# The last low part of the fetched weights written behind the copies of the turned exponentials, in five steps of the attention over the neighbourhoods

## The chip, the core and the metric

The kernel runs on one core of a Trainium2 chip. The metric is the device time of one execution in microseconds (us). Names of engines: PE is TensorE's matmul side and PEld its weight loads, DVE is VectorE, ACT is ScalarE, POOL is GpSimd, SP is SyncE, which issues the weight transfers.

## The reference

Two layers of a transformer over 256 latent tokens and 256 context tokens of width 1024: the first mixes with a retention, the second with attention over neighbourhoods, and each is followed by a squared-ReLU MLP. The change lies in the second layer's attention: 32 heads of 32, the latent tokens on a grid of 4 rows by 64 columns, each query with 8 x 16 neighbours at most (here all 4 rows) and all 256 context tokens. Cut to what matters:

```python
q = p[..., :d].reshape(b, rows, GRID_W, nh, hd) * scale
s_loc = jnp.einsum('bqhd,bikhd->bhqik', q_r, k_band).astype(jnp.float32) + bias
s_ctx = jnp.einsum('bqhd,blhd->bhql', q_r, k_c).astype(jnp.float32)
s = jnp.concatenate([s_loc.reshape(b, nh, GRID_W, band), s_ctx], axis=-1)
prob = jax.nn.softmax(s, axis=-1).astype(v.dtype)
o = (jnp.einsum('bhqik,bikhd->bqhd', p_loc, v_band)
     + jnp.einsum('bhql,blhd->bqhd', prob[..., band:], v_c))
y_lat = o.reshape(b, n, d) @ w_o
```

## The kernel before

**Split operands.** Matmul operands of 32-bit floats are held as two parts: a high part that ScalarE casts (`hi`) and a low part that VectorE makes as the difference (`lo = raw - hi`). A product is then three matmuls: high by high, high by low, low by high (`mm3`).

**Weights.** They come in units of 512 KB in a fixed order. `fetch(n)` (line 255) issues the transfers of the next n units on SP into one of four `raw` buffers and writes the ScalarE casts of their high parts at once; the VectorE subtractions are put on a list, `pending`. `lows(n)` (line 277) writes the first n of that list. `take(n)` (line 282) hands units to a product. A `raw` buffer comes free when its subtraction has run, and SP's queue, which runs in order, waits for that before a later transfer. There are five buffers each for high and low parts.

**Banks.** PSUM has eight banks, handed out by `bank()` (line 156). One is held for the attention's sums (`pav`); the other seven serve in turn the scores (`pqk`, four a step), the projections (`pn`, `pnv`, `pnw`) and the transposes (`ppt`, four a step). A matmul into a bank waits until the evacuation of its former contents has run.

**The order.** PE, ACT and DVE run in the order in which the code is written (`ORDER`, line 1396); SP too. The attention goes over sixteen pairs n of a head group and a half of the queries; the loop at line 1825 has thirteen steps, and step n works on three pairs at once:

- `gather(n + 1)` on POOL: small copies of exponentials, and the transfers of bias rows; `turned(n)`: an ACT copy of the inverted sums.
- `scores(n + 2)` on PE: twelve score matmuls into four banks.
- `soften(n + 2)`: on DVE, four times, the bias added and the extreme found (`s`, `mn`), then on ACT four exponentials with their sums.
- `fetch(late)` and `lows(late)`: up to two units of weights.
- `run(before)`: a projection: K gives `kT` (ACT casts its high part, DVE subtracts for the low one), Q gives `qT` the same way in two pieces, V is copied by ACT, W is the output projection (`pnw`).
- `flip(n + 1)`: thirteen transposes of the exponentials on PE into four banks, which ACT (first and third) and DVE (second and fourth) copy to `pt`, 384 or 512 columns each.
- `invert(n + 2)` on DVE: reciprocal of the sums and its spread (`rr`).
- `fetch(last)`, then `attend(n)`: PE multiplies `pt` with V into `pav`, DVE scales it (`rt`), ACT casts the high part `oTh`, DVE subtracts for `oTl`. At the end of a step what is left on the list is written.

The table `STEPS` (line 1805) gives each step its numbers early, late and last and its projections: steps 1, 2 and 4 have late = 2 with K(3), K(4) and Q(2), step 3 has late = 1 with K(5), and step 9 has late = 2 with Q(3) and K(6). Step 5 has late = 1 with V(0).

Of the kernel before, what the change touches and what calls it, by code (L numbers as in the profile page):

```python
# [104 lines left out]
def kernel(  # L105
# [46 lines left out]
    def nm(s):  # L152
        uid[0] += 1
        return f"{s}_{uid[0]}"

    def bank(s="ps"):
        return psp.tile([P, 512], F32, tag="ps", name=nm(s))
# [8 lines left out]
    def tsl(t):  # L166
        return slice(t * P, (t + 1) * P)
# [87 lines left out]
    def fetch(n, in_scratch=False, at=None):  # L255

        for src, k, ncol in specs[len(units) : len(units) + max(n, 0)]:
            raw = rawp.tile([P, k, ncol], F32, tag="raw", name=nm("raw"))
            sp.dma_start(out=raw[:], in_=src.rearrange("(k p) n -> p k n", p=P))
            if in_scratch or len(units) in scratch_units:  # L260
                hi, lo = Rows([scr("hi", F32R) for _ in range(k)]), Rows([scr("lo", F32R) for _ in range(k)])
                for i in range(k):
                    act.copy(out=hi[:, i, :], in_=raw[:, i, :])
                    pending.append((lo[:, i, :], raw[:, i, :], hi[:, i, :]))
                units.append((hi, lo))
                continue
            if at is None:
                hi = hip.tile([P, k, ncol], F32R, tag="hi", name=nm("hi"))
                lo = lop.tile([P, k, ncol], F32R, tag="lo", name=nm("lo"))
            else:  # L270
                both = slot(at, [P, 2, k, ncol], F32R, "hilo")
                hi, lo = both[:, 0], both[:, 1]
            act.copy(out=hi[:], in_=raw[:])
            pending.append((lo[:], raw[:], hi[:]))
            units.append((hi, lo))

    def lows(n=100, eng=None):
        for lo, raw, hi in pending[:n]:
            (eng or dve).tensor_sub(out=lo, in0=raw, in1=hi.bitcast(F32))
        del pending[:n]  # L280

    def take(n, ahead=WB, open_=0):
        first = taken[0]
        while len(units) < min(first + max(n, ahead), len(specs)):
            fetch(1)
            lows()
        taken[0] = first + n
        assert len(units) - len(pending) >= first + n - open_
        return units[first : first + n]
# [987 lines left out]
    for hf in range(2):  # L1277
# [65 lines left out]
        for half in range(2):  # L1343
# [24 lines left out]
            held = take(4)  # L1368
# [174 lines left out]
    def scores(n):  # L1543

        g, qt = n // 2, n % 2
        pss[n] = [bank("pqk") for _ in range(4)]
        q, k = q_of(g), kTs[g // 2][:, g % 2]
        for i, (a, b) in enumerate(((0, 0), (0, 1), (1, 0))):
            for j in range(4):
                js = slice(32 * j, 32 * j + 32)  # L1550
                pe.matmul(
                    pss[n][j][:], lhsT=q[js, a, tsl(qt)], rhs=k[js, b, :], start=(i == 0), stop=(i == 2),
                    tile_position=(32 * j, 0),
                )

    def soften(n):

        mn = smp.tile([P, 4], F32, tag="mn", name=nm("mn"), bufs=3)
        sm = sums[n] = smp.tile([P, 4], F32, tag="sums", name=nm("sums"), bufs=3)
        for j in range(4):  # L1560
            s = Es[n, j] = scr("s")
            dve.tensor_tensor_reduce(
                out=s[:].rearrange("p (a t) -> p a t", a=2),
                in0=pss[n][j][:].rearrange("p (a t) -> p a t", a=2),
                in1=bias_ap(n, j),
                scale=1.0,
                scalar=3.0e38,
                op0=ALU.add,
                op1=ALU.min,
                accum_out=mn[:, j : j + 1],  # L1570
            )
            act.activation(
                out=s[:], in_=s[:], func=AF.Exp, scale=-1.0, bias=mn[:, j : j + 1], accum_out=sm[:, j : j + 1]
            )
# [7 lines left out]
    def invert(n):  # L1582

        rr = rrs[n] = smp.tile([P, 4, HD], F32, tag="rr", name=nm("rr"), bufs=1)
        dve.reciprocal(out=sums[n][:], in_=sums[n][:])
        dve.tensor_copy(out=rr[:], in_=sums[n][:].unsqueeze(2).broadcast_to([P, 4, HD]))
# [6 lines left out]
    def pt_at(n, i):  # L1593
        return turns[n % 2][:, tsl(i)]

    def gather(n):

        o = 0 if n % 2 else P
        c0 = 24 if n % 2 else 0
        for j in range(4):  # L1600
            pool.tensor_copy(
                out=pt_at(n, RAW)[:, 32 * j : 32 * j + 32].rearrange("p (r c) -> p r c", r=4),
                in_=Es[n, j][:, o : o + P].rearrange("p (r c) -> p r c", r=4)[:, :, c0 : c0 + 8],
            )
        if n + 2 < NS:
            load_bias(n + 2)

    def flip(n, sums_too=True):
        for j in range(4):
            pp = bank("ppt")  # L1610
            for i, kc in enumerate((n % 2, 2, 3)):
                pe.transpose(pp[:, tsl(i)], Es[n, j][:, tsl(kc)], ident)
            w = 3 * P
            if j == 3:
                pe.transpose(pp[:, tsl(3)], pt_at(n, RAW), ident)
                w = 4 * P
            (dve.tensor_copy if j % 2 else act.copy)(
                out=turns[n % 2][:, 3 * j * P : 3 * j * P + w], in_=pp[:, :w]
            )
        if sums_too:  # L1620
            flip_sums(n)

    def flip_sums(n):
        pe.transpose(av_half(n)[:, P:], rrs[n][:].rearrange("p h d -> p (h d)"), ident)
# [4 lines left out]
    def turned(n):  # L1629

        rts[n] = smp.tile([P, P], F32, tag="rt", name=nm("rt"), bufs=2)
        act.copy(out=rts[n][:], in_=av_half(n)[:, P:])

    def attend(n):

        g, qt = n // 2, n % 2
        oTh, oTl = oTs[0]
        po, rt = av_half(n), rts[n]
        pe.matmul(po[:, :P], lhsT=rest_values(n), rhs=pt_at(n, NEAR), start=True, stop=False)
        for i, kc in enumerate((qt, 2, 3)):  # L1640
            for j in range(4):
                pe.matmul(
                    po[32 * j : 32 * j + 32, :P],
                    lhsT=vtile(kc, g // 4)[:, (4 * (g % 4) + j) * HD : (4 * (g % 4) + j + 1) * HD],
                    rhs=pt_at(n, 3 * j + i),
                    start=False,
                    stop=(i == 2),
                    tile_position=(0, 32 * j),
                )
        dve.tensor_mul(out=rt[:], in0=po[:, :P], in1=rt[:])  # L1650
        hi, lo = (
            o[:, g].rearrange("p (r b c) -> p r b c", r=4, b=2)[:, :, qt] for o in (oTh, oTl)
        )
        split(rt[:].rearrange("p (r c) -> p r c", r=4), hi, lo)
# [166 lines left out]
    def run(fs):  # L1821
        for f in fs:
            f()

    for n, (early, late, last, before, after) in enumerate(STEPS):
        gather(n + 1)
        turned(n)
        fetch(early)
        lows(early)
        scores(n + 2)  # L1830
        soften(n + 2)
        fetch(late)
        lows(late)
        run(before)
        flip(n + 1)
        invert(n + 2)
        fetch(last)
        attend(n)
        run(after)

        lows(100 if n < len(STEPS) - 2 else len(STEPS) - 1 - n)


    n = NS - 1
# [263 lines left out]
    held = {}  # L2108
# [105 lines left out]
```

## Time and profile before

| | us |
|---|---|
| three runs | 1179.67, 1178.79, 1179.38; median 1179.38 |
| the profiled execution | 1179.48 |
| its span, first to last instruction | 1177.4 |
| mean granted TensorE clock, share of full speed | 0.998 |
| step 2, from flip to flip (859.33 to 868.44) | 9.11 |
| step 3 (868.44 to 877.72) | 9.28 |
| step 4, with the two pieces of Q (877.72 to 887.74) | 10.02 |
| step 5 (887.74 to 897.36) | 9.62 |
| step 6 (897.36 to 906.50) | 9.14 |

Times in the profile count from the start of the span. The span is that of one execution; about 2.1 us lie around it. In a timeline a row has the start, the length of the row, the engine, the operation, what it writes and reads (out<-in) and how many instructions follow each other (x), and in brackets the idle time of the engine before it with what ended that. A row of several instructions is as long as all of them. Reads of an accumulator are left out of what is shown. A stage above starts with the transposes of one flip and ends with those of the next, so it holds the scores and the projection of the step that gives it its name.

### The profile page before, as it was taken

The numbers are of one execution on the slowest core, as the hardware profiler recorded it, in microseconds if no ns is written. First come the engines' busy times: TensorE is split into PE (matmuls) and PEld (weight loads), VectorE is DVE, ScalarE is ACT, GpSimd is POOL, SyncE is SP. The second block draws the span as 40 slices with busy tenths as digits, with TensorE's granted clock in tenths as the row PEclk, the third lists the DMA queues.
The fourth block names the chain that finished last, engine by engine and source line by source line (L and its number), as shares of the span: only waits on it lengthen the run. The fifth ranks groups of instructions, "written<-read, shape, count | busy, mean of one in ns | idle before, by whom it ended". The sixth has DMA issues, their size and how long they took to land.

```text
span 1177.4 us, 17745 instructions
## 1 busy us (share of the span) xinstructions
PE 1167.3 (99%) x6821; PEld 985.6 (84%) x6821; DVE 844.6 (72%) x1349; ACT 480.6 (41%) x819; POOL 212.5 (18%) x364
## 2 busy tenths in 40 slices
PE   9999999999999999999999999999999999999997
PEld 7788888888888889888888888889888878999886
DVE  3786678787888787757767675678577589877446
ACT  3643332222323246442212333137466666665341
POOL 0103001000200241780203000223343430000001
PEclk9999999999999999999999999999999999999999
DMA  9943544544355416757566665646344334766660
GB/s 276 276 130 104 161 143 140 152 147 152 118 169 175 141 60 214 189 112 217 171 190 197 212 199 190 201 141 204 83 135 139 111 115 155 222 209 197 233 212 36
DMA packets 140115, 195.10 MB, mean 166 GB/s; under 512 B 9936, under 2 KB 81136, under 8 KB 140032
## 3 DMA queue, kind: packets, MB, share of 16 engines
q1 hardware_dynamic: 131904, 182.03, 49.4%
q0 software_dynamic: 6976, 9.39, 3.9%
q10 hardware_dynamic: 1152, 2.56, 0.7%
q8 instruction: 53, 0.87, 0.3%
q14 instruction: 30, 0.25, 0.1%
HBM read 189.12 MB, written 5.75 MB: 166 GB/s over the span
## 4 chain that ended last, share of the span: by engine, by line
PE 94%; DMA 2%; SPq 1%; ACT 1%; DVE 1%; issue 0%; POOL 0%; ACTq 0%; DVEq 0%
PE p L84 44%; PE pw L84 7%; PE pg L84 7%; PE pq L84 7%; PE pv L84 7%; PE pn L84 5%; PE pnv L84 4%; PE po L84 3%; PE ppt L84 2%; PE pnw L84 1%; PE pS L84 1%; PE pav L84 1%; PE pqk L84 1%; SPq L84 1%; PE pt L84 1%; PE p1t L84 1%
## 5 line engine op out<-in xcount | busy, mean ns | idle before, releaser
L84 ACT CAST hi<-raw 128x1024 fp32r<-128x1024 f32 (+2 forms) x228 | 231.7, 1032 | 308.9 <-PE p L84 113.4
L84 DVE TENSOR_TENSOR lo<-raw,hi 128x1024 fp32r<-128x1024 f32 (+2 forms) x228 | 273.4, 1213 | 105.5 <-ACT hi L84 105.4
L84 PE MATMUL p<-hi,hid 128*128 128x512 f32 (+1 forms) x832 | 241.8, 373 | 0.0
L84 PEld LDWEIGHTS p<-hi,hid 128*128 128x128 f32 x832 | 152.1, 188 | 27.6
L84 PE MATMUL p<-hTh,lo 128*128 128x256 f32 (+1 forms) x512 | 165.8, 326 | 0.0
L84 PE MATMUL p<-hTl,hi 128*128 128x256 f32 (+1 forms) x512 | 165.8, 326 | 0.0
L84 PE MATMUL p<-hTh,hi 128*128 128x256 f32 (+1 forms) x512 | 162.9, 328 | 0.0
L84 PE MATMUL p<-lo,hid 128*128 128x512 f32 (+1 forms) x416 | 155.2, 373 | 0.0
L84 DVE SCALAR_TENSOR_TENSOR acc<-rawa,scol,acc 128x1024 f32<-128x1024 f32 x56 | 74.5, 1342 | 66.0 <-DMA rawa<-in_ada_w_dram 66.0
L84 PEld LDWEIGHTS p<-hTh,lo 128*128 128x128 f32 x512 | 96.4, 188 | 8.8
L84 PEld LDWEIGHTS p<-hTl,hi 128*128 128x128 f32 x512 | 96.4, 188 | 8.7
L84 PEld LDWEIGHTS p<-hTh,hi 128*128 128x128 f32 x512 | 94.2, 188 | 8.7
L84 PEld LDWEIGHTS p<-lo,hid 128*128 128x128 f32 x416 | 78.4, 188 | 13.7
L84 DVE SCALAR_TENSOR_TENSOR strips<-rawa,scol,strips 128x512 f32<-128x512 f32 x112 | 78.6, 762 | 0.0
L84 ACT CAST hid<-r 128x256 fp32r<-128x256 f32 (+1 forms) x64 | 31.9, 500 | 111.2 <-DVE r L84 111.2
L84 POOL TENSOR_TENSOR rstd<-rstd,misc 128x1 f32<-128x1 f32 x28 | 19.1, 684 | 212.4 <-DVE rstd L84 211.4
L84 POOL TENSOR_TENSOR R<-R,acc 128x512 f32<-128x512 f32 x16 | 25.8, 1633 | 168.8 <-DVE acc L84 168.8
L84 ACT ACTIVATE s<-s,mn 128x512 f32<-128x512 f32 x64 | 45.5, 713 | 22.0 <-DVE mn L84 22.0
L84 PE MATMUL pw<-hi,oh 128*128 128x512 f32 x128 | 51.0, 398 | 0.0
L84 PE MATMUL pg<-hi,hTh 128*128 128x512 f32 x128 | 50.6, 395 | 0.0
L84 PE MATMUL pq<-hTh,hi 128*128 128x512 f32 x128 | 49.3, 395 | 0.8 <-ACT hTh L84 0.5
L84 PE MATMUL pw<-hi,ol 128*128 128x512 f32 x128 | 49.9, 390 | 0.0
(238 smaller groups left out, 2278.5 us busy)
## 6 DMA issues: line engine op xcount, KB each, us to landing
raw<-in_mlp_w_dram SPq DMA_DIRECT2D x128, 512.0 KB, 4.2
rawa<-in_ada_w_dram SPq DMA_DIRECT2D x80, 512.0 KB, 3.9
raw<-in_ret_w_in_dram SPq DMA_DIRECT2D x42, 512.0 KB, 3.9
raw<-in_nat_w_in_dram SPq DMA_DIRECT2D x24, 512.0 KB, 4.3
rawq<-in_ada_w_dram SPq DMA_DIRECT2D x16, 512.0 KB, 6.2
raw<-in_ret_w_o_dram SPq DMA_DIRECT2D x16, 512.0 KB, 3.4
bias<-rpb_rows POOLq DMA_DIRECT2D x32, 128.0 KB, 2.9
raw<-in_nat_w_o_dram SPq DMA_DIRECT2D x8, 512.0 KB, 3.8
```

Of the source, the lines that this page charges most:

```text
L84: r = f(*args, **kwargs)
```

## The change

The loop's body writes the last low part of `late` not before the projection and the transposes, but behind `flip`, ahead of `invert`. That holds for the steps with late = 2 and for step 3: steps 1, 2, 3, 4 and 9.

```diff
@@ -1830,9 +1830,11 @@
         scores(n + 2)
         soften(n + 2)
         fetch(late)
-        lows(late)
+        held = (late == 2 or n == 3) and late > 0
+        lows(late - held)
         run(before)
         flip(n + 1)
+        lows(int(held))
         invert(n + 2)
         fetch(last)
         attend(n)
```

On PE, ACT, POOL and SP each instruction stands where it stood. On DVE, step 2 (the rows from the end of its soften to its invert; `lo` of the second unit, `kT` of K(4), the two copies of `flip`):

```order
 L84 ISA mn_7453 128x1
 L84 TENSOR_TENSOR lo_7470<-raw_7467,hi_7469 128x1024
+L84 TENSOR_TENSOR kT_7478<-pn_7479,kT_7478 128x512
+L84 COPY pt_6947<-ppt_7511 128x384
+L84 COPY pt_6947<-ppt_7521 128x512
 L84 TENSOR_TENSOR lo_7475<-raw_7472,hi_7474 128x1024
-L84 TENSOR_TENSOR kT_7479<-pn_7480,kT_7479 128x512
-L84 COPY pt_6947<-ppt_7512 128x384
-L84 COPY pt_6947<-ppt_7522 128x512
 L84 RECIPROCAL sums_7454<-sums_7454 128x4
 L84 COPY rr_7529<-sums_7454 128x128
```

The second subtraction moved from ahead of kT to ahead of the reciprocal. Steps 1 and 3 are alike (step 3 has no other low ahead of kT), and in step 4 two pieces of `qT` stand in kT's place.

On DVE, step 9, where the projections Q(3) and K(6) both stand between:

```order
 L84 TENSOR_TENSOR lo_8340<-raw_8337,hi_8339 128x1024
+L84 SCALAR_TENSOR_TENSOR qT_6598<-pn_8348,qT_6598 128x256
+L84 SCALAR_TENSOR_TENSOR qT_6598<-pn_8349,qT_6598 128x256
+L84 TENSOR_TENSOR kT_8402<-pn_8403,kT_8402 128x512
+L84 COPY pt_6946<-ppt_8435 128x384
+L84 COPY pt_6946<-ppt_8445 128x512
 L84 TENSOR_TENSOR lo_8345<-raw_8342,hi_8344 128x1024
-L84 SCALAR_TENSOR_TENSOR qT_6598<-pn_8349,qT_6598 128x256
-L84 SCALAR_TENSOR_TENSOR qT_6598<-pn_8350,qT_6598 128x256
-L84 TENSOR_TENSOR kT_8403<-pn_8404,kT_8403 128x512
```

The subtraction `lo_8345` now follows qT, kT and both copies; it is the low part of the first unit that the output projection of step 10 reads. The next row on DVE is the reciprocal, and behind it come `rt`, `oTl` and the low part of the second such unit, `lo_8459`.

On PE, the scores that open step 6 in the changed kernel (before, the same but for a number), with the semaphores that each waits for:

```order
L84 MATMUL pqk_7946<-kT_7478,qT_6598 128x512 [waits DVE_49]
L84 MATMUL pqk_7947<-kT_7478,qT_6598 128x512 [waits DVE_49]
L84 MATMUL pqk_7948<-kT_7478,qT_6598 128x512 [waits Activation_49]
L84 MATMUL pqk_7949<-kT_7478,qT_6598 128x512 [waits Activation_49]
L84 MATMUL pqk_7946<-kT_7478,qT_6598 128x512
```

The first two go into banks that VectorE's soften has read, the third and the fourth into banks that ScalarE copies out of: that of the V projection of step 5 (copied to `R`) and that of the first transposes.

## The prediction

> **What bounds the kernel now.** First the page: which engine is busy, and what the chain that ended last is made of.
>
> ```profile
> PE 1167.3 (99%) x6821; PEld 985.6 (84%) x6821; DVE 844.6 (72%) x1349; ACT 480.6 (41%) x819; POOL 212.5 (18%) x364
> PE 94%; DMA 2%; SPq 1%; ACT 1%; DVE 1%; issue 0%; POOL 0%; ACTq 0%; DVEq 0%
> ```
>
> TensorE has hardly a gap, so a reordering on VectorE pays or costs only where TensorE waits. Second, the timeline of TensorE's weight loads, to find such waits in the thirteen steps. Each step opens with twelve score matmuls (pqk). Below are the groups that open steps 2, 3, 4 (in two rows), 5, 6 and 10.
>
> ```profile
> 862.19 0.54 PEld L84 LDWEIGHTS pqk<-kT,qT 32*128 32x128 f32 x12 [0.20 <-issue]
> ...
> 871.31 0.68 PEld L84 LDWEIGHTS pqk<-kT,qT 32*128 32x128 f32 x12 [0.20 <-issue]
> ...
> 880.59 0.19 PEld L84 LDWEIGHTS pqk<-kT,qT 32*128 32x128 f32 x3 [0.20 <-DVE lo L84]
> 881.10 0.52 PEld L84 LDWEIGHTS pqk<-kT,qT 32*128 32x128 f32 x9 [0.33 <-DVE kT L84]
> ...
> 890.48 1.17 PEld L84 LDWEIGHTS pqk<-kT,qT 32*128 32x128 f32 x12 [0.20 <-DVE lo L84]
> ...
> 900.23 0.54 PEld L84 LDWEIGHTS pqk<-kT,qT 32*128 32x128 f32 x12 [0.20 <-issue]
> ...
> 943.18 0.54 PEld L84 LDWEIGHTS pqk<-kT,qT 32*128 32x128 f32 x12 [0.20 <-ACT hi L84]
> ```
>
> A free group takes 0.54. Steps 3, 4 and 5 take 0.14, 0.49 (881.10 + 0.52 less 880.59 and 0.54) and 0.63 more: TensorE waits for banks that late evacuations still hold. These 1.26 us are all that TensorE loses around the five edited places; the other groups, step 10's too, are free. Third, who is late: VectorE's timeline through steps 1 to 4, and where its lateness ends.
>
> ```profile
> 858.93 2.36 DVE L84 TENSOR_TENSOR lo<-raw,hi 128x1024 fp32r<-128x1024 f32 x2 [2.17 <-ACT hi L84]
> 861.21 0.68 DVE L84 TENSOR_TENSOR kT<-pn,kT 128x512 fp32r<-128x512 f32 x1
> ...
> 864.64 0.69 DVE L84 CUSTOM_DVE_ANT_1 s<-pqk,bias 128x512 f32<-128x512 f32 x1 [0.41 <-DMA G<-rpb_rows]
> ...
> 869.27 2.36 DVE L84 TENSOR_TENSOR lo<-raw,hi 128x1024 fp32r<-128x1024 f32 x2 [2.10 <-ACT hi L84]
> 871.55 0.68 DVE L84 TENSOR_TENSOR kT<-pn,kT 128x512 fp32r<-128x512 f32 x1
> 872.15 1.14 DVE L84 COPY pt<-ppt 128x384 f32<-128x384 f32 x2
> 873.21 0.17 DVE L84 RECIPROCAL sums<-sums 128x4 f32<-128x4 f32 x1
> ...
> 874.27 0.29 DVE L84 TENSOR_TENSOR oTl<-rt,oTh 128x128 fp32r<-128x128 f32 x1 [0.37 <-ACT oTh L84]
> 874.58 0.69 DVE L84 CUSTOM_DVE_ANT_1 s<-pqk,bias 128x512 f32<-128x512 f32 x1
> ...
> 879.22 1.23 DVE L84 TENSOR_TENSOR lo<-raw,hi 128x1024 fp32r<-128x1024 f32 x1 [2.11 <-ACT hi L84]
> 880.36 0.68 DVE L84 TENSOR_TENSOR kT<-pn,kT 128x512 fp32r<-128x512 f32 x1
> ...
> 888.05 2.36 DVE L84 TENSOR_TENSOR lo<-raw,hi 128x1024 fp32r<-128x1024 f32 x2 [2.11 <-ACT hi L84]
> 890.33 0.75 DVE L84 SCALAR_TENSOR_TENSOR qT<-pn,qT 128x256 fp32r<-128x256 f32 x2
> ...
> 894.46 0.68 DVE L84 CUSTOM_DVE_ANT_1 s<-pqk,bias 128x512 f32<-128x512 f32 x1
> ...
> 907.59 0.56 DVE L84 COPY pt<-ppt 128x384 f32<-128x384 f32 x1 [2.37 <-PE ppt L84]
> ```
>
> The reader is to see a loop: soften (s), a wait of about 2.1 for ScalarE, lows, kT, the copies, reciprocal, oTl, and at once the next soften. Step 3's scores begin at 871.31 and are softened only from 874.58, step 5's (890.48) from 894.46. So in steps 2 to 5 VectorE, with ScalarE between, is the late partner, and TensorE is its customer; only at 907.59 does VectorE wait for TensorE again. Whatever makes this loop longer before that shows at TensorE.
>
> **The change, part by part.** Nothing is added or removed: five subtractions of 1.23 move behind kT (or qT) and the two copies. No DMA is issued elsewhere. What decides is whether kT can start in the freed slot. It needs ScalarE's half first:
>
> ```profile
> 859.76 0.58 ACT L84 CAST kT<-pn 128x512 fp32r<-128x512 f32 x1
> ...
> 870.10 0.57 ACT L84 CAST kT<-pn 128x512 fp32r<-128x512 f32 x1
> ...
> 879.10 0.58 ACT L84 CAST kT<-pn 128x512 fp32r<-128x512 f32 x1
> ...
> 888.88 0.64 ACT L84 ACTIVATE qT<-pn 128x256 fp32r<-128x256 f32 x2
> ...
> 895.19 0.72 ACT L84 ACTIVATE s<-s,mn 128x512 f32<-128x512 f32 x1 [1.94 <-DVE mn L84]
> ...
> 898.97 0.57 ACT L84 COPY R<-pnv 128x512 f32<-128x512 f32 x1
> 899.44 0.85 ACT L84 COPY pt<-ppt 128x384 f32<-128x384 f32 x2
> ...
> 940.75 0.59 ACT L84 CAST kT<-pn 128x512 fp32r<-128x512 f32 x1 [2.42 <-PE pn L84]
> ```
>
> One low takes a slot of 1.14 (879.22 to 880.36). In step 1 VectorE would be free for kT at 858.93 + 1.14 = 860.07, but the cast ends at 860.34; with 0.03 to hand over (940.75 + 0.59 to a start at 941.36 is 0.02) kT starts at 860.37. So 0.30 of idle time enters that the second low used to fill. Step 2: 870.41 against 870.70, 0.29. Step 3, whose only low is held: 879.22 against 879.71, 0.49. Step 4: 889.19 against about 889.28 (the first of two activates, estimated to end at 889.25), 0.09. Sum 1.17. kT and the copies come 0.65 to 0.85 earlier, yet the low still has to run before the reciprocal, so everything from there on is later by the idle time: reciprocal, rt, oTl, and the next soften, for which ScalarE's exponentials, high parts, kT cast and copies wait. Each lag is handed to the next step, since the loop has no other slack, with one doubtful exception: the 0.41 of idle before 864.64 might swallow step 1's 0.30. I take it as not swallowed, because the bias rows that this soften reads were fetched a step before the transfer that the row names; swallowed, the sum is 0.87.
>
> What TensorE makes of it: the stalls of steps 4 and 5, which end with kT and qT, shrink; step 3's ends with a ScalarE copy or kT and stays or grows. But the gain is lent. In step 6 the third and fourth score matmuls wait for ScalarE copies, by the order of banks the R copy and the first pt copy. Now these end at 899.54 and about 899.9 (the first of two in 0.85, an estimate), just before the 900.23 at which the group starts. They lie behind the softened scores of step 5 (the row at 895.19 waits for VectorE), so they move by 1.17: 901.07, and with 0.06 from an evacuation's end to the matmul (kT 880.36 + 0.68 to 881.10) 901.13. TensorE starts the fourth score 0.9 later than now, however early it arrives. Term one: +0.9. The bounds: with no idle time at all the 1.26 of stalls are gained; with every slot of 1.14 exposed in steps 1 to 4 the lag is 4.56 and the term 899.9 + 4.56 + 0.06 - 900.23 = +4.3. It is nearest to the rows of the casts, which lie 0.1 to 0.5 behind, not 1.14.
>
> Step 9 is a place of its own:
>
> ```profile
> 936.86 2.36 DVE L84 TENSOR_TENSOR lo<-raw,hi 128x1024 fp32r<-128x1024 f32 x2 [2.11 <-ACT hi L84]
> ...
> 941.36 0.69 DVE L84 TENSOR_TENSOR kT<-pn,kT 128x512 fp32r<-128x512 f32 x1 [1.48 <-ACT kT L84]
> ...
> 943.03 0.17 DVE L84 RECIPROCAL sums<-sums 128x4 f32<-128x4 f32 x1
> ...
> 944.30 1.22 DVE L84 TENSOR_TENSOR lo<-raw,hi 128x1024 fp32r<-128x1024 f32 x1
> ...
> 945.81 0.39 PE L84 MATMUL pnw<-lo,oTh 128*128 128x512 f32 x1
> ```
>
> Here two projections stand before kT, so kT waits 1.48 for TensorE and ScalarE anyway. The second low at 936.86 is free now; taking it out frees nothing, and behind the copies it takes its whole slot: the reciprocal moves from 943.03 to 944.17, and the low of the following unit from 944.30 to 945.44, ending at 946.66. The output projection of step 10 reads that low at 945.81, now 0.29 after its end. It would start at 946.72: +0.91. The held low itself, read by the same product, ends in time within 0.1. VectorE is then 1.14 late and TensorE 0.91, and the difference of 0.23 can return at step 10's softening; from 0 to 0.23 I take 0.2. Below, this place costs nothing only if VectorE gained 0.9 before it, which nothing in its rows offers; above, 1.14.
>
> A held low also holds its raw buffer longer, and the fetch queue waits for lows:
>
> ```profile
> SPq L84 <- DVE lo L84: 153.9, 21, 30.4
> ```
>
> These fetches come 2 to 6 us later, but no ScalarE cast of a high part between 840 and 1000 waits for a transfer, and waits up to 30.4 in the fetch queue already end in time. Cost 0.
>
> Sum: 0.9 + 0.9 + 0.2 = +2.0 on the profiled 1179.48 (span 1177.4 and 2.1 around it), which lies 0.1 above the median 1179.38 of the three runs: **1181.5**. After step 10 TensorE has no slack in which to catch up. The Trainium skill, "VectorE: DVE Perf Modes", section "The DRAIN you can't avoid", says that a semaphore between two Vector ops costs nothing extra. Here an op behind another starts 0.08 before that one's end (869.27 + 2.36 to 871.55), one behind a wait 0.02 after it; by the rule the first three idle times would each lose about 0.1 and the time would be 1181.2.
>
> **The rivals.** (B) One place pays alone: the 0.41 at 864.64 swallows lag, or step 6's copies have more room than read. Then step 9's 0.91 and a remainder stay, about 1180.5. Against it: the soften follows oTl without a gap everywhere else. (C) Not slower: the stalls are the whole story. With kT and qT 0.65 to 0.85 earlier the 1.26 vanish and step 6 has the room: 1178.2; it decides if the R and pt copies at 898.97 do not move. For it stand the two rows that name DVE lo and DVE kT at TensorE's wait; against it that 894.46 follows VectorE's own queue. The Trainium skill, "Perfetto Trace Analysis", section "Optimization Strategy", advises just that: find the gap on the most contended engine and let what it waits for start sooner. By that rule the change should give this result; the rows of the loop speak against it. (D) Slower by more: casts come later within the changed loop than the rows now show, so that held lows expose more than the idle time read off, up to the slot; two further half slots on the way to step 6 make 1182.6, the upper bound of all 1179.48 + 4.3 + 1.1 = 1184.9. It decides if kT's cast moves against VectorE's lag. (E) The moved lows change nothing, 1179.5: excluded, as the five places do change on VectorE.
>
> **How the numbers follow.** Forecast 0.66, B 0.09, C 0.08, D 0.17. What this kernel's measurement can tell from no change is about 0.2%, 2.4 us, so 1181.74 is the line, and the forecast lies 0.25 under it. Its terms are read from handovers of hundredths but through two engines and six steps; I give it 1180.9 to 1182.3 of its own and put 0.31 of its 0.66 above the line. Slower: 0.31 + 0.17 = 0.48. Faster by over 2.4 would need more than every stall: 0.03, out of C. Same: the rest, 0.49. The range leaves out C and the far part of D: 1179.9 to 1183.0.
>
> **What would show it.** Right: kT on VectorE with idle time ended by ScalarE's kT in steps 1 to 3; the score groups of steps 4 and 5 shorter than 1.0 and 1.17; step 6's group longer by 0.6 or more, ended by ScalarE; a gap of about 0.9 before pnw in step 10, ended by a low. Wrong: step 6's group still 0.54 with R copied by 899.6 (C), softens that follow within the old distances (B), or idle times of over 0.7 before kT (D).

## The result, and the profile after

| kernel | median us | runs | lowest to highest |
|---|---|---|---|
| before | 1179.24 | 14 | 1178.61 to 1181.71 |
| changed | 1181.12 | 14 | 1180.53 to 1184.44 |

The measured ratio is 1.002 with a 95% interval of 1.0011 to 1.0028 (the quotient of the two medians is 1.0016; the ratios below are not quotients of medians either): the change makes the kernel slower by about 1.9 us (1181.12 - 1179.24), 0.16%. The profiled execution took 1181.35 us, with a span of 1179.3.

The page of the changed kernel: its span, the busy shares, and the shares of the chain of work that ended last.

```profile
span 1179.3 us, 17740 instructions
...
PE 1168.4 (99%) x6821; PEld 986.9 (84%) x6821; DVE 845.2 (72%) x1349; ACT 480.5 (41%) x819; POOL 212.5 (18%) x364
...
PE 96%; DVE 2%; ACT 1%; DMA 1%; issue 1%; POOL 0%; DVEq 0%; ACTq 0%
```

No engine's work grew: busy time is the same within 1.3 us on each, as it must be when instructions only change places. The loss is in waits, and the page can't show which. The timeline of TensorE's weight loads can (start, duration, engine, line, operation, count, idle time before it and what ended that). First the group of step 0, then those that open steps 3, 4, 5 and 6, the row behind the last, the output projection and the transposes of step 10:

```profile
843.73 0.54 PEld L84 LDWEIGHTS pqk<-kT,qT 32*128 32x128 f32 x12 [0.35 <-issue]
...
871.08 0.25 PEld L84 LDWEIGHTS pqk<-kT,qT 32*128 32x128 f32 x3 [0.20 <-issue]
871.50 0.52 PEld L84 LDWEIGHTS pqk<-kT,qT 32*128 32x128 f32 x9 [0.17 <-DVE kT L84]
...
880.60 0.71 PEld L84 LDWEIGHTS pqk<-kT,qT 32*128 32x128 f32 x12 [0.20 <-issue]
...
890.17 0.18 PEld L84 LDWEIGHTS pqk<-kT,qT 32*128 32x128 f32 x1 [0.20 <-DVE lo L84]
890.57 0.85 PEld L84 LDWEIGHTS pqk<-kT,qT 32*128 32x128 f32 x11 [0.22 <-DVE qT L84]
...
900.05 0.18 PEld L84 LDWEIGHTS pqk<-kT,qT 32*128 32x128 f32 x2 [0.20 <-issue]
900.50 0.18 PEld L84 LDWEIGHTS pqk<-kT,qT 32*128 32x128 f32 x1 [0.27 <-ACT R L84]
900.87 0.52 PEld L84 LDWEIGHTS pqk<-kT,qT 32*128 32x128 f32 x9 [0.19 <-ACT pt L84]
901.76 0.19 PEld L84 LDWEIGHTS pnv<-hi,hTh 128*128 128x128 f32 x1 [0.36 <-DVE pt L84]
...
947.32 0.19 PEld L84 LDWEIGHTS pnw<-lo,oTh 128*128 128x128 f32 x1 [1.16 <-DVE lo L84]
...
948.36 1.46 PEld L84 LDWEIGHTS ppt<-cst,s 128*128 128x128 f32 x12
```

The same places of the kernel before, in the same view (its groups of steps 3 to 6 stand in the prediction):

```profile
843.96 0.54 PEld L84 LDWEIGHTS pqk<-kT,qT 32*128 32x128 f32 x12 [0.35 <-issue]
...
901.14 0.19 PEld L84 LDWEIGHTS pnv<-hi,hTh 128*128 128x128 f32 x1 [0.37 <-DVE pt L84]
...
946.73 1.46 PEld L84 LDWEIGHTS ppt<-cst,s 128*128 128x128 f32 x12
```

Two profiled executions don't begin alike. At step 0, ahead of every edit, the changed kernel is 0.23 us earlier (843.73 - 843.96). That offset is added to every later difference, and what remains is the **shift** that the edits cause. Behind the group of step 6 it is 901.76 - 901.14 + 0.23 = +0.85; at the transposes of step 10 it is 948.36 - 946.73 + 0.23 = +1.86. Worked out in this way for the row behind each score group, and for every kernel that ran:

| kernel (offset at step 0) | step 2 | 3 | 4 | 5 | 6 | 10 | 11 | last |
|---|---|---|---|---|---|---|---|---|
| changed (-0.23) | 0 | +.27 | -.07 | +.01 | **+.85** | +.85 | **+1.89** | +1.97 |
| steps 1 to 4 alone (-0.91) | 0 | +.29 | -.04 | +.04 | +.89 | +.95 | +.93 | +.95 |
| step 9 alone (+0.58) | 0 | 0 | 0 | 0 | 0 | 0 | +1.01 | +1.09 |
| step 4 alone (-0.75) | 0 | 0 | 0 | **-.63** | -.19 | -.19 | -.21 | -.19 |
| two lows past the next soften (-0.76) | 0 | 0 | -.50 | -1.13 | -1.14 | -1.16 | -1.18 | -1.15 |
| lows right behind kT (+1.97) | 0 | +.32 | -.01 | +.06 | +.93 | +.96 | +.94 | +.96 |
| step 9, low between Q(3) and K(6) (-0.57) | 0 | .02 to .07 throughout | | | | | | +.05 |

The last column is the first matmul behind step 12 (p1t). "0" stands for 0.03 or less. Two places carry the loss, the group of step 6 and the output projection of step 10.

VectorE of the changed kernel: kT in steps 1, 2 and 3 with the wait before it, the softens of steps 2, 3, 4 and 5, the two qT pieces of step 4, and kT of step 9.

```profile
860.15 0.69 DVE L84 TENSOR_TENSOR kT<-pn,kT 128x512 fp32r<-128x512 f32 x1 [0.22 <-ACT kT L84]
...
864.69 0.69 DVE L84 CUSTOM_DVE_ANT_1 s<-pqk,bias 128x512 f32<-128x512 f32 x1 [0.38 <-DMA G<-rpb_rows]
...
870.75 0.69 DVE L84 TENSOR_TENSOR kT<-pn,kT 128x512 fp32r<-128x512 f32 x1 [0.20 <-ACT kT L84]
...
874.93 0.69 DVE L84 CUSTOM_DVE_ANT_1 s<-pqk,bias 128x512 f32<-128x512 f32 x1
...
880.05 0.69 DVE L84 TENSOR_TENSOR kT<-pn,kT 128x512 fp32r<-128x512 f32 x1 [2.58 <-ACT kT L84]
...
884.23 0.69 DVE L84 CUSTOM_DVE_ANT_1 s<-pqk,bias 128x512 f32<-128x512 f32 x1
...
890.10 0.76 DVE L84 SCALAR_TENSOR_TENSOR qT<-pn,qT 128x256 fp32r<-128x256 f32 x2
...
895.37 0.68 DVE L84 CUSTOM_DVE_ANT_1 s<-pqk,bias 128x512 f32<-128x512 f32 x1
...
941.97 0.69 DVE L84 TENSOR_TENSOR kT<-pn,kT 128x512 fp32r<-128x512 f32 x1 [2.52 <-ACT kT L84]
```

The waits that end with ScalarE's kT are new: 0.22, 0.20, and 0.47 (the 2.58 takes the place of the 2.11 that VectorE waited there for hi). In step 9 the wait before kT only grew, from 1.48 to 2.52: the slot that the low left became idle time. Against the kernel before (864.64, 874.58, 883.41 and 894.46) the four softens come later by 0.28, 0.58, 1.05 and 1.14, the offset added: the lag rises by 0.28, 0.30, 0.47 and 0.09 from step to step, and none of it is made up in these steps. ScalarE's copies that step 6 waits for, that to R and those of the first and third transposes (two in a row; before: 898.97 and 899.44), carry it on: with the offset they start 1.14 and 1.15 later.

```profile
899.88 0.57 ACT L84 COPY R<-pnv 128x512 f32<-128x512 f32 x1
900.36 0.84 ACT L84 COPY pt<-ppt 128x384 f32<-128x384 f32 x2
```

The low part that the output projection of step 10 waits for ends at 947.27, 0.05 before the matmul at 947.32; before, it started at 944.30.

```profile
946.05 1.22 DVE L84 TENSOR_TENSOR lo<-raw,hi 128x1024 fp32r<-128x1024 f32 x1
```

### The profile page after: what moved, and what is told of

Its sections match the earlier page's. It is cut to its first block, busy times and chain, and to the rows that moved or that the text cites. A ratio compares the mean times of both kernels' runs of the same rounds, so it can differ in the third digit from the quotient of the medians.

```text
span 1179.3 us, 17740 instructions
## 1 busy us (share of the span) xinstructions
PE 1168.4 (99%) x6821; PEld 986.9 (84%) x6821; DVE 845.2 (72%) x1349; ACT 480.5 (41%) x819; POOL 212.5 (18%) x364
## 4 chain that ended last, share of the span: by engine, by line
PE 96%; DVE 2%; ACT 1%; DMA 1%; issue 1%; POOL 0%; DVEq 0%; ACTq 0%
PE p L84 44%; PE pq L84 8%; PE pv L84 7%; PE pg L84 7%; PE pw L84 7%; PE pn L84 5%; PE pnv L84 4%; PE po L84 3%; PE pnw L84 1%; PE pS L84 1%; PE ppt L84 1%; PE pada L84 1%; PE pav L84 1%; PE pqk L84 1%; PE pt L84 1%; PE p1t L84 1%
## 5 line engine op out<-in xcount | busy, mean ns | idle before, releaser
L84 PE MATMUL pg<-hi,hTl 128*128 128x512 f32 x128 | 49.9, 390 | 0.0
```

The lines of the kernel that those rows point to most:

```text
L84: r = f(*args, **kwargs)
```

## The experiments

Times come from two batches, each on one chip with its own runs of the kernel before: a median of 1179.16 (33 runs) for the first four kernels, 1180.07 (23 runs) for the last two. With 11 or 12 runs each, intervals are 1.0 to 1.4 us to either side. The shift in the trace tells apart what the times can't.

**Steps 1 to 4 alone.** The low of step 9 stays where it was (this diff and the next are against the kernel before).

```
-        lows(late)
+        held = n in (1, 2, 3, 4)
+        lows(late - held)
         run(before)
         flip(n + 1)
+        lows(int(held))
         invert(n + 2)
```

> The change in steps 1 to 4 alone, step 9 as before. Lag theory (VectorE idles before kT, 0.2 to 0.5 us a step, and hands the lag on until TensorE waits for ScalarE's copies in step 6): +0.9 us against before (0.7 to 1.1), the score group of step 6 longer by 0.6 to 0.9. Stall rival (only the waits of steps 3 to 5 count): -0.6 to -1.3 us. Third view, all of the change's cost lies in step 9: 0.0 us.

Measured: 1179.76, ratio 1.0009 (1.0000 to 1.0017): +0.60 by the medians, a little under what was expected, with an interval that can't tell. The shift is +0.89 at step 6 and +0.95 at the end. The group of step 6 in its timeline of weight loads:

```profile
899.36 0.18 PEld L84 LDWEIGHTS pqk<-kT,qT 32*128 32x128 f32 x2 [0.20 <-issue]
899.85 0.18 PEld L84 LDWEIGHTS pqk<-kT,qT 32*128 32x128 f32 x1 [0.31 <-ACT R L84]
900.22 0.53 PEld L84 LDWEIGHTS pqk<-kT,qT 32*128 32x128 f32 x9 [0.19 <-ACT pt L84]
```

The first two matmuls start when TensorE gets there; the third waits for ScalarE's copy to R, the fourth for its copy to pt. The shift through step 5 is nearly nothing, so the whole loss of these four edits is in these two waits.

**Step 9 alone.** The edit is the one above with `n == 9` for the four steps.

> The change in step 9 alone. Lag theory: +1.1 us against before (0.9 to 1.2), with TensorE waiting about 0.9 us before the second pnw product of a low part in step 10, and the stalls of steps 3 to 5 as before. Rival, the cost of step 9 is only a share of what steps 1 to 4 carry over: under 0.3 us. Together with the run of steps 1 to 4 it should make the +1.9 us of the whole change.

Measured: 1180.04, +0.88 by the medians, ratio 1.0012 (1.0003 to 1.0021). The group of step 6 is free again, and the wait in step 10 is there:

```profile
900.80 0.53 PEld L84 LDWEIGHTS pqk<-kT,qT 32*128 32x128 f32 x12 [0.20 <-issue]
...
947.26 0.19 PEld L84 LDWEIGHTS pnw<-lo,oTh 128*128 128x128 f32 x1 [1.19 <-DVE lo L84]
```

The shift is +1.09 at the end. With the +0.95 of the other part that makes 2.04, against 1.97 for the whole change: two losses that simply add up. By the medians it is 0.60 + 0.88 = 1.48 against 1.88, which the intervals allow.

**Step 4 alone.** The edit with `n == 4`. It is the one of the four whose slot is nearly filled by qT (0.09 of idle time by the prediction), and so the one where making TensorE's wait end sooner should pay, if that is what counts.

> The change in step 4 alone, where the cast of qT ends only about 0.1 us behind the freed slot. Lag theory: next to no idle time is added, and the stall of step 5 shrinks from 0.63 to about 0.4 us: -0.1 to -0.3 us against before. Stall rival: the whole stall goes, -0.6 us. If each held low costs about the same whatever the idle time before kT: +0.2 us.

Measured: 1179.03, ratio 1.0 (0.9991 to 1.0009); shift -0.63 behind the group of step 5, -0.19 from step 6 to the end. Its weight loads for steps 5 and 6, then ScalarE's copy to R between them:

```profile
889.73 0.54 PEld L84 LDWEIGHTS pqk<-kT,qT 32*128 32x128 f32 x12 [0.20 <-issue]
...
898.87 0.25 PEld L84 LDWEIGHTS pqk<-kT,qT 32*128 32x128 f32 x3 [0.20 <-issue]
899.31 0.52 PEld L84 LDWEIGHTS pqk<-kT,qT 32*128 32x128 f32 x9 [0.19 <-ACT pt L84]
```

```profile
898.31 0.57 ACT L84 COPY R<-pnv 128x512 f32<-128x512 f32 x1
```

The stall of step 5, 0.63 before, is gone entirely; it was expected to shrink to 0.4, with nothing handed back. That the net -0.19 lies in the expected range is luck. One step later 0.44 is handed back: TensorE arrives 0.63 early at a bank whose copy has not moved (898.31 against 898.97 before, less the offset of 0.75: 0.09 later). This is the run that separates the two theories. Had the stall been the whole story, the shift would have stayed at -0.63.

**The low past the next soften.** Also against the kernel before: in steps 2 and 3 one low is left over, and done behind the following step's soften, where VectorE waits about 2.1 us for ScalarE's high part.

```
         soften(n + 2)
+        lows(int(n - 1 in (2, 3)))
         fetch(late)
-        lows(late)
+        held = n in (2, 3)
+        lows(late - held)
         run(before)
...
-        lows(100 if n < len(STEPS) - 2 else len(STEPS) - 1 - n)
+        if not held:
+            lows(100 if n < len(STEPS) - 2 else len(STEPS) - 1 - n)
```

> Not the change: the last low part of steps 2 and 3 is held further, until behind the softening of the next step, where VectorE waits about 2.1 us for ScalarE anyway; all else as before. Lag theory: VectorE's loop gets shorter by a slot of 1.14 us in each of two steps, the stalls of steps 3 to 5 (1.26 us) nearly vanish and step 6 stays free: -1.0 to -1.25 us against before. Rival, where a low stands does not matter so long as kT comes first: +0.3 to +0.9 us, like the change.

Measured: 1178.13, ratio 0.9986 (0.9977 to 0.9995), 1.0 us faster than the kernel before in the same batch. Its weight loads at steps 4, 5 and 6, and VectorE from the held low of step 2 on:

```profile
879.82 0.54 PEld L84 LDWEIGHTS pqk<-kT,qT 32*128 32x128 f32 x12 [0.20 <-issue]
...
889.23 0.53 PEld L84 LDWEIGHTS pqk<-kT,qT 32*128 32x128 f32 x12 [0.20 <-issue]
...
898.34 0.53 PEld L84 LDWEIGHTS pqk<-kT,qT 32*128 32x128 f32 x12 [0.20 <-issue]
```

```profile
875.45 1.22 DVE L84 TENSOR_TENSOR lo<-raw,hi 128x1024 fp32r<-128x1024 f32 x1
878.11 0.69 DVE L84 TENSOR_TENSOR kT<-pn,kT 128x512 fp32r<-128x512 f32 x1 [1.45 <-ACT kT L84]
...
892.21 0.68 DVE L84 CUSTOM_DVE_ANT_1 s<-pqk,bias 128x512 f32<-128x512 f32 x1
```

The low at 875.45 runs in time that was idle before: the 2.11 ahead of step 3's low is now 1.22 of work and 1.45 of waiting. The loop gets shorter, and step 5's soften comes 1.49 earlier than before (894.46 - 892.21, less the offset of 0.76). ScalarE's copy to R moves with it, so step 6 takes nothing back: its group takes 0.53, although TensorE arrives over 1.1 earlier. The stalls of steps 4 and 5 are gained and kept; step 3's 0.14, which was expected to go as well, stays.

**Right behind kT.** The held lows of steps 1 to 4 between kT (qT) and the two copies, instead of behind the copies (shown against the edit of steps 1 to 4 above).

```
         run(before)
+        lows(int(held))
         flip(n + 1)
-        lows(int(held))
         invert(n + 2)
```

> Steps 1 to 4, the held low right behind kT (or qT) and ahead of the transposes' copies; step 9 as before. Lag theory: the idle time before kT is what costs, and it is the same: +0.7 to +1.0 us against before, idle time before kT in steps 1 to 3 as in the run with the low behind the copies (0.2, 0.2 and about 2.6 us, of which 2.1 stood there before). Rival, it is the low's place between the copies and the reciprocal that delays the next softening: 0.0 us.

Measured: 1180.26, ratio 1.0001 (0.9989 to 1.0012), which by itself tells nothing. The shift is that of steps 1 to 4 alone in every column, +0.96 against +0.95 at the end. So it does not matter where between kT and the reciprocal the low stands; that it no longer stands ahead of kT is what costs.

**Step 9, between Q(3) and K(6).** The low of step 9 behind qT, but ahead of kT, which waits there anyway.

```
-        (2, 2, 1, [Q(3), K(6)], []),
+        (2, 2, 1, [Q(3), lambda: lows(1), K(6)], []),
...
-        lows(late)
+        lows(late - (n == 9))
```

> In step 9 the held low stands between qT and kT, where VectorE waits 1.48 us for ScalarE; the other steps as before. Lag theory: the low runs inside that wait and nothing behind kT moves: 0.0 us against before (under 0.2), no wait of TensorE for a low part in step 10. Rival, any move of that low past the projection Q costs, through its buffers or the first product that reads it: +0.5 to +1.1 us.

Measured: 1179.57, ratio 0.9997 (0.9986 to 1.0008); shift +0.05 at the end. VectorE in step 9:

```profile
937.59 0.76 DVE L84 SCALAR_TENSOR_TENSOR qT<-pn,qT 128x256 fp32r<-128x256 f32 x2
938.26 1.22 DVE L84 TENSOR_TENSOR lo<-raw,hi 128x1024 fp32r<-128x1024 f32 x1
940.87 0.69 DVE L84 TENSOR_TENSOR kT<-pn,kT 128x512 fp32r<-128x512 f32 x1 [1.39 <-ACT kT L84]
```

The wait before kT takes up the low, whether it stands at the front of it or behind qT. Only past kT does the low have no cover.

## Why the prediction was right, point by point

- **The lag of VectorE's loop: right.** 0.30, 0.29, 0.49 and 0.09 were read off the rows of ScalarE's casts; 0.28, 0.30, 0.47 and 0.09 came. The sum of 1.14, against 1.17, reaches the soften of step 5 whole. The printed idle times are smaller, 0.22 and 0.20, since an operation behind a wait also loses the 0.08 by which it would otherwise overlap its forerunner. The rule of the Trainium skill that was weighed there ("VectorE: DVE Perf Modes", section "The DRAIN you can't avoid": a semaphore between two Vector operations costs nothing extra) would have made the first three 0.20, 0.19 and 0.39. The trace shows more at each of the three places. What the Trainium skill gives there was measured on Vector operations with semaphores between them; these three wait for ScalarE, and to them it does not carry over. The times (1181.12, against 1181.5 and 1181.2) can't tell.
- **The 0.41 of idle time at 864.64 as a cushion: rightly not counted.** The changed kernel still waits 0.38 there, and the soften comes 0.28 later. So what ends this wait comes later by as much as the loop; which transfer or engine it is was not settled. Rival B falls.
- **Term one, +0.9 at step 6: right, and its mechanism too.** The fourth score was put 0.27 short of the lag of 1.17, for the room that the copies have before TensorE arrives. By the runs that room is 1.14 - 0.85 = 0.29 in the changed kernel, and 0.09 + 0.63 - 0.44 = 0.28 with step 4 alone, where TensorE comes early instead of the copies late.
- **"The gain is lent", on the way there: wrong in its size, without effect on the sum.** The prediction let kT and the copies come 0.65 to 0.85 earlier in all four steps (by its own rows 1.05 for qT of step 4, 890.33 - 889.28), and so the stalls of both steps 4 and 5 shrink. That left out the lag that it had itself added up. With the offset added, kT comes 0.83 earlier in step 1 (860.15 against 861.21), 0.57 in step 2, 0.08 in step 3, and qT of step 4 not at all (890.10 + 0.23 against 890.33). Step 4's group did get shorter, from 1.0 to 0.71, but step 5's did not: 1.25 (890.57 + 0.85 - 890.17), against 1.17. So one of the signs named beforehand failed. Nothing hung on it, because step 6's copies set TensorE's time however early it arrives; the shift at step 5, +0.01, shows that there was no gain left to lend.
- **Step 3's stall grew by 0.26, as allowed for, and what ends it changed.** The row of the changed kernel names kT of VectorE, and rightly: kT ends at 871.44 and the fourth score is loaded at 871.50, 0.06 later, as at the other waits for a bank. ScalarE's copies of pt end at 871.47, only 0.03 before:

```profile
870.62 0.85 ACT L84 COPY pt<-ppt 128x384 f32<-128x384 f32 x2
```

  Before the change this can't have been the wait: kT ended at 872.23 there, and the group's loads were over at 871.99. So kT comes 0.57 earlier and delays a matmul that did not wait for it before. The reason is the bank. In the kernels as built, the fourth score of step 3 goes into a bank of step 2's transposes, which ScalarE empties, before the change, and into that of step 2's K projection, which kT empties, after it. The banks are not handed out strictly in turn; moving the low changed the choice. In step 6 it is the same in both kernels: the bank of the V projection and one that ScalarE copies pt out of.
- **Step 9, +0.91: right.** The matmul that reads the low starts at 947.32, against 945.81 before: +1.74 with the offset, of which 0.85 was there already, so 0.89.
- **The last +0.2, at step 10's softening: nearly the size by luck, with another cause.** The shift is 1.74 at the waiting matmul, and already 1.86 at the transposes, ahead of anything that the softening releases. Between them stand only the waiting matmul and four that wait for nothing. Here are the one ahead of the wait and the waiting one itself on TensorE:

```profile
946.21 0.39 PE L84 MATMUL pnw<-hi,oTh 128*128 128x512 f32 x1
947.32 0.50 PE L84 MATMUL pnw<-lo,oTh 128*128 128x512 f32 x1 [0.72 <-DVE lo L84]
```

  Behind the wait the matmul takes 0.50 where one in a row takes 0.39: 0.11 of the 0.12. The step that failed is "the difference of 0.23 can return at step 10's softening": the score groups of steps 11 and 12 take 0.56 and 0.54, before 0.54 each, so VectorE's further lateness shows in none of them, and breaking the row of matmuls cost 0.1 instead. With step 9 alone the same comes out: 947.26 - 945.81 - 0.58 = 0.87 at the wait, and 1.01 behind the next score group.
- **Rival C (the stalls are the whole story) falls twice:** steps 1 to 4 alone are +0.95, not -1.26, and step 4 alone gives back 0.44 of the 0.63 that it gains. Its price of 1178.2 also left out the 0.91 of step 9, which does not hang on the stalls; with it C would have been 1179.1. The advice of the Trainium skill ("Perfetto Trace Analysis", section "Optimization Strategy") to let what the most contended engine waits for start sooner is half of it: step 4 alone does just that, and keeps 0.19. The low past the next soften also shortens the loop that made it late, and keeps 1.15.
- **The fetch queue, cost 0: right.** Its waits for low parts between 840 and 1000 add up to 157.4 in place of 153.9 and are no longer than 30.1; there as before, no cast of a high part waits for a transfer.

```profile
SPq L84 <- DVE lo L84: 157.4, 23, 30.1
```

- **Rival D (slower by more) has nothing for it:** no new wait before kT is over 0.7, apart from step 9's, which was priced as a whole slot.

The sum was +2.0; the trace has 0.85 + 0.89 + 0.12, with 0.11 that creeps in behind, with step 9 alone too (1.01 to 1.09), and is not explained: 1.97, and the medians of the runs +1.88.

## What to carry to other kernels

Work that is moved behind an operation on a late engine is free only if that operation can already start. Here kT's other half, on a third engine, came 0.1 to 0.5 us after the freed slot began, and each such gap entered a loop without slack and stayed in it. TensorE, with hardly a gap, was served by shortening the loop that feeds it, not by serving one of its waits sooner: the wait filled from idle time kept its gain (1.15 us), the one served by reordering handed 0.44 of 0.63 back a step later. For each step one should ask for which copy the engine will wait if it comes early, and after an edit ask again, since the banks may be other ones.

## What the runs showed of the hardware

- TensorE's wait in step 10 cost 0.11 more than its length: the 128x512 matmul behind it took 0.50 and the next one started 0.34 after it (947.32 to 947.66); in a row they take 0.39 and start 0.23 apart (945.81 to 946.04 before).
- From the end of an evacuation to the matmul that waits for its bank 0.05 to 0.06 us pass, whether VectorE empties it (kT, 871.44 to 871.50) or ScalarE (R, 900.45 to 900.50).
- On VectorE a row's printed idle time understates what a new wait costs, by up to 0.1: 0.22 and 0.20 printed, 0.28 and 0.30 of lag.
- At the row behind step 2's scores, where no edit has had an effect yet, all eight profiled executions agree within 0.03 us once the offset is taken off, but as wholes they don't: the offset at step 0 went from -0.91 to +1.97, and single runs of one kernel differ by up to 5.8 us (1178.48 to 1184.29, the kernel before in the second batch). What varies lies outside the thirteen steps. The execution profiled with step 4 alone was the longest of its 11 (1181.34, median 1179.03), although its shift is -0.19: it falls back by 2.9 us between 1005 and 1082, in the last MLP, with 657 matmuls in that window where the kernel before has 678, at the same granted clock of 1.00. The execution with the lows right behind kT falls back by 2.7 us at 770. Why is open.
